# Expanding cached latents by plain fp32 products instead of three split ones, in a decoder step

## Chip, cores and metric

One core of one Trainium2 chip runs the whole program. The time is device microseconds of an execution; three runs of the kernel before are given, and one further execution was profiled.

## What is computed

Two trunk layers of a hybrid decoder are run for 256 prompt tokens and for 8 samples of 8 new tokens each (320 tokens in all). A layer has four mixers side by side (A: latent attention, B: convolution, C: spatial gating, D: a delta-rule recurrence), then cross attention to a memory, then a gated feed-forward. The change lies in mixer A of the samples. There every new query looks at a cache of 2048 past positions, kept as pages of 128 latent rows with 128 numbers each:

```
def mla_expand(ckv, p):
    k_nope = rmsnorm((ckv @ p['mla_w_uk']).reshape(*lead, MLA_HEADS, QK_NOPE), p['mla_gk_nope'])
    v = (ckv @ p['mla_w_uv']).reshape(*lead, MLA_HEADS, V_DIM)
...
    def page_step(carry, phys):
        kn_p, v_p = mla_expand(ckv_p, p)
        sp = mla_scores(q_nope, q_pe, kn_p, kpe_p)
        m_new = jnp.maximum(m, jnp.max(sp, axis=-1, keepdims=True))
...
```

The keys of a page are the latents times a 128x256 matrix, normalised for each head of 64. Only the norms need that product itself: the scores are taken from the latents directly, by queries that were multiplied with the same matrix once.

## The kernel before

The program is written through a framework whose scheduler orders the instructions of each engine from their dependences and its own estimates; each engine then works through its list in that order, and semaphores hold it where a result is missing. `in_order` (L380) keeps the big dense products in their written order, `hold` (L387) keeps an instruction back in the schedule alone.

Dense products use a split: a number is kept as a high part (an fp32r cast, ScalarE) and a low part (the rest, VectorE or GpSimd), and a product is the sum of high by high, high by low and low by high, each a fast fp32r product (`split`, L479; `dense_T`, L513). Activations are split once for each norm in `norm_pre` (L562): for each of the 8 column blocks of the residual stream `x`, one tile `h` of high and low parts (names Nh, Xh and Fh in the profile: before the mixers, before the cross attention, before the feed-forward; six norms in two layers).

The scan over the cache is `mla_sample` (L1298). It has 8 steps a layer: four rounds over the pages, each for two groups of 4 samples. For one step `scan` (L1311) does this:

- It loads 16 page numbers into registers of SP, and SP then issues 16 loads of 64 KB: four tiles `ckt` of 128 x 512 (Sckt in the profile: the latents, transposed, of four pages of one sample). The ring has 12 such tiles, three steps. GpSimd gathers the same pages as rows by four indirect loads (Scb).
- For each of the four tiles ScalarE makes the high part (Sckh, L1336) and GpSimd the low part (Sckl, L1337).
- For each half `u` of the 256 key columns and each tile `j`, three products into a bank pS make the expansion, and ScalarE squares it into Ssq (L1350). The weights uh and ul (Auk) are the split key matrix, made once a layer (L1301 to L1304).
- Narrow products (pZ, L1353) sum the squares over each head: weights of 128 x 32, the squares as 512 moving columns. Each writes 32 of the 128 partitions, so the four tiles `j` fill four quarters of PE's columns and can run at once.
- Four more narrow products (pZ, L1356) of the same form give the scores, from queries and the unsplit Sckt.
- Logarithm, exponentials and a correction step (Sz, Sra; ScalarE and VectorE) turn the sums into inverse norms and scale the scores.

```
                for j in range(4):
                    mm(pn[32 * j : 32 * j + 32], C("hsum")[:, 32 * u : 32 * u + 32], sqs[j], u == 0, u == 1)
            p = ps("Z")
            for j in range(4):
                mm(p[32 * j : 32 * j + 32], qf(4 * g + j), cks[j])
```

`attend` (L1402) then adds the rotary part of the scores (pA from Scb), takes the running softmax, transposes the weights (pA from Sra) and multiplies them with the page rows (pA from Scb and Ak). The scan of the next step is written ahead of the attend of this one, and side work is put between steps: the convolution (Bkeep, pE), the spatial gating (Ccv) and the ends of the other mixers. Banks of PSUM: three for pS, two for pZ, two for pK (the memory's keys and values, `mem_proj`, L1459, which loads memT and weights through the ring wr of three tiles on SP's queue).

## Time and profile before

| | |
|---|---|
| median of 3 runs | 1381.34 us |
| lowest, highest | 1374.33, 1381.94 us |
| span of the profiled execution | 1383.1 us |
| PE, VectorE, ScalarE, GpSimd busy | 1330.9, 962.2, 651.6, 217.5 us |
| the two scans | 191 to 333 us, 886 to 1029 us |
| the two feed-forward stretches | 484 to 716 us, from 1150 us |

The profiled execution has no time of its own beside its span, which runs from the program's first to its last instruction; the span stands 1.8 us above the median of the runs. In the profile a plain fp32 product shows as two records, an fp32r product as one. A record's length includes the way through the array, so records overlap, and the rate of products is read from the distance of their starts.

### The profile page before, as it was taken

How to read it: one execution, taken by the hardware profiler on the slowest of the kernel's cores; microseconds unless marked ns; L12 is line 12 of the kernel's file. 1: busy time of each engine (PE TensorE's matmuls, PEld its weight loads, DVE VectorE, ACT ScalarE, POOL GpSimd, SP SyncE). 2: the span in 40 equal slices, each digit the busy share in tenths (PEclk: the TensorE clock that was granted, in tenths of full speed). 3: DMA queues.
4: the chain of work that ended last, by engine and by line, in shares of the span. 5: the costliest groups of instructions: out<-in, count | busy, mean ns of one | idle time of the engine just before them, and what ended most of it. 6: DMA issues, size and time to landing. Idle time of an engine off the chain costs nothing.

```text
span 1383.1 us, 25248 instructions
## 1 busy us (share of the span) xinstructions
PE 1330.9 (96%) x9032; PEld 1113.5 (81%) x9032; DVE 962.2 (70%) x2414; ACT 651.6 (47%) x1425; POOL 217.5 (16%) x280
## 2 busy tenths in 40 slices
PE   5999999999999999999999899999999989999998
PEld 5859765566796799999998597755668959999998
DVE  6879468767786666566786894698777957655663
ACT  4443236667554544434444432375674635442441
POOL 1201313553000000000012113135540000000000
PEclk9999799999999999999999997999999999999999
DMA  7320313454475544444652204134563823444433
GB/s 233 125 77 15 118 44 89 140 159 145 146 253 191 177 157 145 154 153 151 201 171 94 81 11 123 42 88 133 162 215 143 296 93 137 147 144 153 153 115 107
DMA packets 105486, 189.52 MB, mean 137 GB/s; under 512 B 21393, under 2 KB 58642, under 8 KB 105362
## 3 DMA queue, kind: packets, MB, share of 16 engines
q1 hardware_dynamic: 91040, 157.84, 34.6%
q0 software_dynamic: 5120, 20.98, 5.0%
q10 hardware_dynamic: 9202, 9.11, 2.3%
q8 instruction: 71, 1.16, 0.3%
q14 instruction: 53, 0.43, 0.1%
HBM read 182.12 MB, written 5.75 MB: 136 GB/s over the span
## 4 chain that ended last, share of the span: by engine, by line
PE 52%; issue 9%; DVE 2%; POOL 1%; DMA 1%; ACT 0%; SPq 0%; POOLq 0%; ACTq 0%
PE pD L375 38%; PE pR L375 5%; PE pS L375 2%; PE pA L375 2%; PE pZ L375 2%; PE pA L460 1%; DMA Sckt<-in_ckvT 1%; PE pR L460 0%; DVE Bkeep L401 0%; DVE u L401 0%; PE pE L460 0%; POOL Sckl L397 0%; DVE Ccv L401 0%; DVE u L397 0%; DVE Sz L401 0%
## 5 line engine op out<-in xcount | busy, mean ns | idle before, releaser
L482 ACT CAST wh<-wr 128x512 fp32r<-128x512 f32 (+1 forms) x448 | 252.4, 601 | 133.0 <-PE pD L375 83.9
L375 PE MATMUL pD<-Fh,wh 128*128 128x320 f32 x1408 | 310.5, 309 | 0.0
L397 DVE TENSOR_TENSOR wl<-wr,wh 128x512 fp32r<-128x512 f32 (+1 forms) x448 | 291.7, 674 | 11.4 <-ACT wh L482 9.8
L375 PEld LDWEIGHTS pD<-Fh,wh 128*128 128x128 f32 x1408 | 235.7, 188 | 0.0
L375 PE MATMUL pD<-Fh,wl 128*128 128x320 f32 x704 | 217.5, 309 | 0.0
L375 PE MATMUL pD<-u,wh 128*128 128x320 f32 x704 | 154.9, 309 | 0.0
L375 PEld LDWEIGHTS pD<-Fh,wl 128*128 128x128 f32 x704 | 132.2, 188 | 0.0
L375 PEld LDWEIGHTS pD<-u,wh 128*128 128x128 f32 x704 | 117.8, 188 | 0.0
L397 DVE TENSOR_TENSOR Ff<-pD,fix 128x320 f32<-128x320 f32 x88 | 43.2, 491 | 103.3 <-PE pD L375 100.9
L375 PE MATMUL pD<-u,wl 128*128 128x320 f32 x352 | 108.8, 309 | 0.0
L375 PE MATMUL pD<-Nh,wh 128*128 128x320 f32 x384 | 94.6, 326 | 13.8 <-ACT wh L482 13.8
L413 ACT ACTIVATE u<-Ff 128x320 fp32r<-128x320 f32 x44 | 20.8, 472 | 176.1 <-DVE Ff L397 176.1
L397 POOL TENSOR_TENSOR Sckl<-Sckt,Sckh 128x512 fp32r<-128x512 f32 x64 | 85.8, 1351 | 108.7 <-ACT Sckh L1336 91.7
L375 PE MATMUL pS<-Sckh,Auk 128*128 128x512 f32 x256 | 92.0, 432 | 4.3 <-DVE Sra L401 1.8
L413 ACT ACTIVATE Ssq<-pS 128x512 f32<-128x512 f32 x128 | 73.5, 594 | 45.3 <-PE pS L375 38.6
L397 DVE TENSOR_TENSOR fix<-fix,pD 128x320 f32<-128x320 f32 x80 | 38.8, 485 | 73.0 <-PE pD L375 72.3
L375 PEld LDWEIGHTS pD<-Nh,wh 128*128 128x128 f32 x384 | 66.8, 194 | 19.6 <-ACT wh L482 13.8
L375 PEld LDWEIGHTS pS<-Sckh,Auk 128*128 128x128 f32 x256 | 47.3, 197 | 36.4 <-issue 22.1
L401 DVE SCALAR_TENSOR_TENSOR Bkeep<-Bkeep,fix 128x256 f32<-128x256 f32 x120 | 74.5, 624 | 0.6
L1326 POOL DMA_INDIRECT Scb<-in_ckv,fix x64 | 63.4, 991 | 63.4 <-PE pR L375 23.3
L375 PE MATMUL pZ<-Ssq,fix 128*32 128x512 f32 x256 | 71.9, 654 | 1.3 <-ACT Sra L414 0.9
L375 PEld LDWEIGHTS pD<-u,wl 128*128 128x128 f32 x352 | 66.1, 188 | 0.0
(478 smaller groups left out, 2580.7 us busy)
## 6 DMA issues: line engine op xcount, KB each, us to landing
wr<-in_w SPq DMA_DIRECT2D x200, 512.0 KB
Sckt<-in_ckvT SPq DMA_DIRECT2D x256, 64.0 KB
u<-in_memK SPq DMA_DIRECT2D x32, 256.0 KB
u<-in_memV SPq DMA_DIRECT2D x32, 256.0 KB
wr<-in_w SPq DMA_DIRECT2D x16, 384.0 KB
wr<-in_memT SPq DMA_DIRECT2D x12, 256.0 KB
wr<-in_w SPq DMA_DIRECT2D x8, 352.0 KB
Rmk<-in_cst ACTq DMA_DIRECT2D x2, 704.0 KB
```

The source lines that it names most:

```text
L375: return T.matmul(out, lhsT=lhsT, rhs=rhs, start=start, stop=stop)
L397: return (eng or V).tensor_tensor(out=out, in0=in0, in1=in1, op=op)
L401: return V.scalar_tensor_tensor(out=out, in0=in0, scalar=scalar, in1=in1, op0=op0, op1=op1)
L413: return S.activation(out, in_, func, bias=bias, scale=scale)
L460: T.transpose(out, in_, ident[:n, :n])
L482: S.copy(hi, src)
L1326: ld = nc.gpsimd.indirect_dma_start(out=cb.rearrange("p i c -> p (i c)"), out_offset=None, in_=a["ckv"], in_offset=off)
```

## The change

In the scan the casts, the low parts, their tiles (Sckh, Sckl) and the split key matrix (Auk) go; each expansion is one plain fp32 product of the unsplit weights `ukv` (in the profile a part of Akeep) and the unsplit tile Sckt. The register loads of a step are held, in the schedule, to the scores of the second step before instead of the low parts of the third. In `norm_pre` the eight tiles of split activations become columns of one tile, and the rings Nh, Fh and Xh have one buffer of eight times the size. Comments and docstrings that the diff also drops are left out here.

```
-    BUFS = dict(u=13, wr=3, wh=4, wl=4, Nh=8, Nf=2, Nsm=2, Fh=8, Ff=4, Fsm=2, Xh=8, Xm=5, Xf=2, Xk2=2, Xcc=2, Xsm=8, Yk2=2, Ycc=2, Ysm=2,
+    BUFS = dict(u=13, wr=3, wh=4, wl=4, Nh=1, Nf=2, Nsm=2, Fh=1, Ff=4, Fsm=2, Xh=1, Xm=5, Xf=2, Xk2=2, Xcc=2, Xsm=8, Yk2=2, Ycc=2, Ysm=2,
...
         hs = []
+        hall = sb("h", [128, 8, 2, NT], F32R)
         for k in range(8):
-            h = sb("h", [128, 2, NT], F32R)
+            h = hall[:, k]
             split(h[:, 0], h[:, 1], x[k], gain[:, k : k + 1])
             hs.append(h)
...
-        u2 = sb("uk", [128, 2, 256], F32R)
-        uh, ul = u2[:, 0], u2[:, 1]
-        hold(S.copy(uh, ukv[:, 0:256]), pages[0])
-        tt(ul, ukv[:, 0:256], uh.bitcast(F32), SUB)
...
-        lows = []
+        base = len(scored)
...
             for ld in loads:
-                hold(ld, lows[-BUFS["Sckt"]] if len(lows) >= BUFS["Sckt"] else cpage)
+                hold(ld, scored[-2] if len(scored) - base >= 2 else cpage)
...
                 ck = ck.rearrange("p n t -> p (n t)")
                 cks.append(ck)
-                hi, lo = sb("ckh", [128, 512], F32R), sb("ckl", [128, 512], F32R)
-                S.copy(hi, ck)
-                lows.append(tt(lo, ck, hi.bitcast(F32), SUB, G if j in [0, 1, 2, 3] else V))
-                ckhl.append((hi, lo))
...
                 for j in range(4):
                     p = ps("F")
-                    hi, lo = ckhl[j]
-                    mm(p, uh[:, us], hi, True, False)
-                    mm(p, ul[:, us], hi, False, False)
-                    mm(p, uh[:, us], lo, False, True)
+                    mm(p, ukv[:, us], cks[j])
                     sq = sb("sq", [128, 512])
                     act(sq, p, AF.Square)
```

The scheduler orders the lists anew. PE, the fifth step of the second layer's scan, before: pS are the expansions, pZ<-Ssq the sums of squares.

```order
L375 MATMUL pS<-Sckh_10949,Auk_10012 128x512 x2
L375 MATMUL pS<-Sckl_10950,Auk_10012 128x512
L375 MATMUL pS<-Sckh_10960,Auk_10012 128x512 x2
L375 MATMUL pS<-Sckl_10961,Auk_10012 128x512
L375 MATMUL pS<-Sckh_10971,Auk_10012 128x512 x2
L375 MATMUL pS<-Sckl_10972,Auk_10012 128x512
L375 MATMUL pS<-Sckh_10982,Auk_10012 128x512 x2
L375 MATMUL pS<-Sckl_10983,Auk_10012 128x512
L375 MATMUL pZ<-Ssq_10991,fix 32x512
L375 MATMUL pZ<-Ssq_10997,fix 32x512
L375 MATMUL pZ<-Ssq_11003,fix 32x512
L375 MATMUL pZ<-Ssq_11009,fix 32x512
```

Here four expansions stand together, and their four narrow products behind them. The same step on PE in the changed kernel; pE belongs to the spatial gating, pK to the memory's keys, pA to the step before, and pZ<-Sckt are the scores:

```order
L375 MATMUL pS<-Sckt_10526,Akeep_9039 128x512
L375 MATMUL pE<-Ccv_10438 128x64 x2
L375 MATMUL pE<-Ccv_10438 64x64 x4
L375 MATMUL pZ<-Ssq_10555,fix 32x512
L375 MATMUL pS<-Sckt_10533,Akeep_9039 128x512
L375 MATMUL pZ<-Sckt_10526,Akeep_9039 32x512
L460 MATMUL pA<-fix,Sra_10198 128x128 x4
L375 MATMUL pS<-Sckt_10540,Akeep_9039 128x512
L375 MATMUL pZ<-Ssq_10559,fix 32x512
L375 MATMUL pZ<-Sckt_10533,Akeep_9039 32x512
L375 MATMUL pZ<-Sckt_10540,Akeep_9039 32x512
L375 MATMUL pK<-wh,Mh_11494 128x512
```

Narrow products stand between the expansions now, one or three at a time, and some of the scores have moved ahead of the sums of squares.

SP's queue in the first layer, at the start of the eighth group of page loads, before (a row ISA sets the address of the load below it):

```order
L1332 DMA Sckt_3455<-in_ckvT 128x128
L1317 TENSOR_LOAD pt_65
L1332 ISA
L1332 DMA Sckt_3757<-in_ckvT 128x128
L1332 ISA
```

The memory's first load follows only behind all of that group. In the changed kernel it stands behind the fourth group, ahead of the fifth:

```order
L1329 DMA Sckt_2597<-in_ckvT 128x128
L1457 DMA wr<-in_memT 128x512
L510 DMA wr<-in_w 128x1024
L1314 TENSOR_LOAD pt_65
L1329 ISA
L1329 DMA Sckt_2793<-in_ckvT 128x128
```

So two loads of the memory's projection were moved past four groups of page loads.

## Rows read from the trace of the kernel before

**Rows 1.** The page: busy us, share of the span and instructions of each engine.

```profile
PE 1330.9 (96%) x9032; PEld 1113.5 (81%) x9032; DVE 962.2 (70%) x2414; ACT 651.6 (47%) x1425; POOL 217.5 (16%) x280
```

**Rows 2.** Stages: window, length, busy us of each engine, granted clock, DMA share, GB/s.

```profile
191.00:333.00 142.00, 135.50 (x950) 81.13 (x949) 109.50 (x261) 91.19 (x214) 64.95 (x60) 0.95 0.42 122
...
886.00:1029.00 143.00, 134.17 (x946) 80.29 (x946) 113.15 (x260) 92.48 (x213) 66.15 (x55) 0.95 0.49 140
```

**Rows 3.** What PE waited for, first scan, then second: us, times, longest.

```profile
PE pS L375 <- DVE Sra L401: 1.0, 1, 1.0
...
PE pS L375 <- ACT Sckh L1336: 0.6, 1, 0.6
...
PE pE L460 <- issue: 0.3, 1, 0.3
...
PE pA L375 <- DVE Ak L1419: 3.2, 1, 3.2
...
PE pE L460 <- issue: 0.2, 1, 0.2
```

**Rows 4.** The chain that ended last, second scan, shares of the window by line.

```profile
by line: PE pS L375 23.5%; PE pZ L375 21.7%; PE pA L375 14.9%; issue 9.6%; DMA Sckt<-in_ckvT 6.3%; DVE Bkeep L401 3.2%; PE pA L460 2.8%; POOL Sckl L397 2.7%; DVE Ccv L401 2.3%; PE pE L460 2.2%; DVE Sz L401 1.5%; SPq L1332 1.3%; DVE Ccv L397
```

**Rows 5.** Timeline of PE, old expansions: start us, us, engine, line, tiles, form, records.

```profile
925.86 0.62 PE L375 MATMUL pS<-Sckh,Auk 128*128 128x512 f32 x2
926.32 0.39 PE L375 MATMUL pS<-Sckl,Auk 128*128 128x512 f32 x1
926.55 0.62 PE L375 MATMUL pS<-Sckh,Auk 128*128 128x512 f32 x2
927.02 0.40 PE L375 MATMUL pS<-Sckl,Auk 128*128 128x512 f32 x1
927.25 0.62 PE L375 MATMUL pS<-Sckh,Auk 128*128 128x512 f32 x2
```

**Rows 6.** Timeline of PE around a plain fp32 product of the new shape.

```profile
83.11 0.40 PE L375 MATMUL pD<-wh,Nh 128*64 128x512 f32 x1
83.34 1.02 PE L375 MATMUL pA<-Akeep 128*128 128x512 f32 x2
83.80 0.80 PE L375 MATMUL pD<-wh,Nh 128*64 128x512 f32 x1
```

**Rows 7.** Timeline of PE, narrow products in groups of four.

```profile
923.21 1.06 PE L375 MATMUL pZ<-Ssq,fix 128*32 128x512 f32 x8
924.10 1.03 PE L375 MATMUL pZ<-Sckt,Akeep 128*32 128x512 f32 x6
```

**Rows 8.** Timeline of PE, a narrow product alone.

```profile
929.32 0.40 PE L375 MATMUL pS<-Sckl,Auk 128*128 128x512 f32 x1
929.71 1.04 PE L375 MATMUL pZ<-Ssq,fix 128*32 128x512 f32 x2
930.69 0.48 PE L375 MATMUL pA<-Akeep,As 64*128 64x128 f32 x2
```

**Rows 9.** Squares, casts, low parts: ns min/median/max, first and last start; then a wait.

```profile
L413 ACT ACTIVATE Ssq<-pS x128: 571/597/616, 194.0 to 1025.0; 128x512 f32<-128x512 f32 x128
L1336 ACT CAST Sckh<-Sckt x64: 600/611/637, 161.5 to 1005.2; 128x512 fp32r<-128x512 f32 x64
L397 POOL TENSOR_TENSOR Sckl<-Sckt,Sckh x64: 1263/1292/1732, 162.2 to 1008.9; 128x512 fp32r<-128x512 f32 x64
...
  DMA Sckt<-in_ckvT: 9.1, 4
```

**Rows 10.** Timeline of VectorE at the start: the low parts of a norm.

```profile
9.95 3.78 DVE L401 SCALAR_TENSOR_TENSOR Nh<-fix,Nh 128x320 fp32r<-128x320 f32 x8
```

More of the change, by code (lines that the diff above doesn't have):

```diff
@@ L1300, in mla_sample @@
         oT = t["take"](4, 64)
-        u2 = sb("uk", [128, 2, 256], F32R)
-        uh, ul = u2[:, 0], u2[:, 1]
-        hold(S.copy(uh, ukv[:, 0:256]), pages[0])
-        tt(ul, ukv[:, 0:256], uh.bitcast(F32), SUB)
         qf = lambda b: qp[:, b].rearrange("p h t -> p (h t)")
         PG = [0, 0, 3, 3]
-        lows = []
+        base = len(scored)
         def scan(g, Q):
             ch[0] = "S"
-            cbs, cks, ckhl = [], [], []
+            cbs, cks = [], []
             cpage = pages[[0, 2, 3, 3][min(2 * Q + g, 3)]]
```

## Prediction, made before the changed kernel ran

> **What bounds the kernel now.** Read the busy shares first: TensorE (PE) is busy 96% of a span of 1383.1 us, VectorE 70%, ScalarE 47%, GpSimd 16% [rows 1]. A busy share says little of what ends a stage, so next come the stages. The change touches two of them, one in each layer: the scan over the cached pages, from 191 to 333 us and from 886 to 1029 us. There PE is busy 135.5 of 142 us and 134.2 of 143 us, and the mean granted clock is 0.95 [rows 2]: between the two levels, 2.4 and 1.2 GHz, that is some 14 us of each scan at the lower one, or 7 us of full-speed time lost in each. Third, what PE itself waited for in these two stretches: nine rows in each, the first and last shown, which add up to 5.6 us in the first and 8.8 us in the second [rows 3]. So about 14 us out of 285 are PE waiting for another engine; the rest is PE working through its list in order, with short gaps where it goes from one kind of product to another. Two things then decide the change: how long PE takes for one expansion by the old and by the new way, and what stands around it in PE's order. The chain that ended last in the second scan says the same: products on pS, pZ and pA hold 60% of it, but 18.6% lie with the page loads, the low parts on GpSimd and gaps in issue [rows 4]; that is the best argument for a rival below.
>
> **The change, part by part.**
>
> *Products.* A scan step expands four tiles of 512 latents by two halves of the key weights: 8 expansions a step, 8 steps a layer, 2 layers, so 128. Each was three products of split (fp32r) operands. Where they follow one another they start at 925.86, 926.55 and 927.25 us: one expansion every 0.69 us [rows 5]. The new one is one plain fp32 product of the same shape, 128x128 weights by 512 columns. The trace has eight records of that shape, two for each product (the new tokens' latents against all 512 columns of the two expansion weights). One starts at 83.34 us; its two records end 1.02 us later, and the next product, 0.80 us long in its record, ends at 84.60 us, while its neighbour of the same kind takes 0.40 us: so it could not begin to stream before 84.20 us. One plain product holds PE for 0.86 us [rows 6]. The difference is 0.17 us, and 128 x 0.17 = 21.8 us more PE time. Bounds: 0 if the new products overlap with their neighbours in a way that these eight records don't show, and 128 x (1.02 - 0.69) = 42 us if nothing can start before the two records have ended. I take 21.8, since the rows are of this very shape.
>
> *Order of PE.* The narrow products (pZ) each fill a quarter of PE's columns. Four side by side take as long as one: eight records, four products, start at 923.21 us and the next four at 924.10, that is 0.89 us [rows 7]. One alone starts at 929.71 us and the next instruction at 930.69 us: 0.98 us [rows 8]. So what counts is not how many there are (96 a layer, before and now) but in how many groups they stand. Counted in PE's order over a scan, where a group is what can run side by side in an unbroken run, there were 35 in each layer; now there are 44 in the first and 48 in the second. The pieces of order printed above show why: the plain expansion is scheduled as one long instruction, and single pZ products are put between expansions. That is 22 groups more, 22 x 0.98 = 21.6 us. Bounds: 0 if each stands where PE would have waited anyway, and 25 us if each also pays the 0.16 us between the end of the wide product before it (929.32 + 0.23 us) and its start. I take 21.6.
>
> The Trainium skill, "TensorEngine Tiling (Array Packing)", Key Properties, says that changing the tiling mode, not merely the tile, drains TensorE. The gaps of 0.16 us ahead of a lone narrow product and 0.12 us behind it agree; by that rule each added group would cost 1.14 us and the sum would be some 3.5 us higher.
>
> *What no longer has to be made.* 64 casts of 611 ns leave ScalarE (39 us) and 64 subtractions of 1.29 us leave GpSimd (83 us) [rows 9], besides two small ones for the weights. Neither engine is the bound: in the scans ScalarE is busy 91 of 142 us and GpSimd 65 [rows 2]. What this pays is only what PE waited for them. Of the waits in [rows 3] one row names the cast, 0.6 us. But ScalarE and GpSimd also feed what VectorE and the squares on ScalarE do, and other rows name those. Bounds: 1 us if only the cast's wait goes, 14.4 us if all of PE's waits in both scans go. I take half, 7.2 us. What is late next is the square of an expansion (597 ns on ScalarE [rows 9]) before its pZ product: one expansion now comes out every 0.86 us instead of 0.69, so squares keep up. Where a lone pZ product does wait for its square, the next expansions stand behind it on PE, and their squares, the scores and the step's softmax behind those.
>
> *Loads.* Each tile of latents is still read by the last pZ product of its step, so buffers of the page loads come free as before. What moves is on SP's queue: in the first layer the first load for the memory's keys (256 KB, and 512 KB of weights behind it) stood behind all eight groups of page loads and stands now behind the fourth. The page loads of four steps are queued behind it. All waits of GpSimd for a page load were 9.1 us in four times [rows 9]; nothing says they reach PE. Bounds: a gain of 9 us to a loss of 9 us; I take nothing. The DMA engines are busy at 0.42 and 0.49 there [rows 2], which is cover enough.
>
> *Split activations in one tile.* The eight splits of a norm write columns of one tile. The first dense products wait for ScalarE and VectorE at the same places in the order as before, so I take nothing. If a product had to wait for all eight, the price would be at most the 3.78 us in which VectorE makes the eight low parts [rows 10], at six norms, 23 us; below nothing there is no reason to go, since the same instructions run.
>
> *Sum.* 21.8 + 21.6 - 7.2 = 36.2 us on a profiled span of 1383.1 us, that is 1419. That span is 1.8 us above the median of the runs, so against the median 1381.3 + 36 = 1417 us.
>
> **The rivals.**
>
> *The added groups are hidden* (0.18). A lone pZ product is put where PE has nothing ready. If it always fills a wait, the 21.6 us fall away: 21.8 - 7.2 = +14.6, 1396 us. For it: the short gaps that PE has at every change of product. Against it: PE's own waits in both scans are 14.4 us in all, fewer than the groups need.
>
> *The split is what paces the scan* (0.09), the case that ends not slower. Place: the head of each step, where a page load lands, is cast, then subtracted, and only then multiplied. In the chain of the second scan the loads, the low parts and the issue gaps hold 6.3 + 2.7 + 9.6 = 18.6% of 143 us, 26.6 us [rows 4]; the same in the first scan makes 53.2. If all that goes, 43.4 - 53.2 = -9.8 us, 1371. It decides as soon as more than 43.4 us of the two scans hang on it. Against it: PE stood still for only 14.4 us of the 285 [rows 3], so most of that chain ran beside PE's work.
>
> *More waits than now* (0.18). Narrow products between wide ones each wait for a square, the memory's loads hold page loads up by the 9.1 us above, and each added group pays its 0.16 us: 36.2 + 9.1 + 3.5 = +48.8, 1430 us. For it: the finer order has more places where PE, which does not reorder products, can wait. Against it: less is asked of ScalarE and GpSimd.
>
> **How the numbers follow.** The forecast, 1417 us, has 0.55. The low end of the range lies under the second case (1396), by some of the 14 us that the lower clock costs in both scans; the high end over the last (1430): 1390 to 1436 us. The runs shown spread by 0.55%, so about 1%, 13.8 us, can be told from no change: below 1367.5 is faster, above 1395.2 slower. Slower takes the forecast, the last rival and two thirds of the second, 0.85; within 1% takes the rest of the second and two thirds of the case of the split, 0.12; faster is what is left of that, 0.03.
>
> **What would show it.** Right: pS has 256 records (two per product) that follow each other by 0.43 us; pZ pairs that stand alone, 0.98 us each, in greater number; both scans longer by some 18 us; the feed-forward stretches, 484 to 716 us and after 1150, as long as before. Wrong: scans of the same length or shorter with PE gaps gone (the split paced them); plain products closer than 0.86 us; longer stages outside the scans (the one tile of activations made products wait, or the clock fell elsewhere); a granted clock in the scans far from 0.95.

## The result and the profile after

The changed kernel takes 1399.39 us (median of 4 runs, 1398.14 to 1405.14) against 1378.58 us for the kernel before in the same comparison (4 runs, 1374.33 to 1381.94): ratio 1.0154, 95% interval 1.0121 to 1.0187, so +20.8 us. The forecast was +36 us, 1417 us, with a range from 1390 to 1436. The profiled execution after has a span of 1397.0 us (its own time 1398.76), 13.9 us over the span of before. The span of before lies 4.5 us above the median of this comparison, so the two profiles show a smaller difference than the runs.

The page of the kernel after, busy us, share of the span and instructions of each engine:

```profile
PE 1353.5 (97%) x8904; PEld 1083.2 (78%) x8904; DVE 925.3 (66%) x2412; ACT 632.4 (45%) x1359; POOL 129.2 (9%) x216
```

Against [rows 1] GpSimd has lost 88 us, 82.7 of them its 64 subtractions, and ScalarE 19 us. VectorE has lost 37 us too, and nothing was taken from it but one small subtraction a layer. That was in nobody's sum, and it turns out to matter.

The stages of the kernel after (window, length, busy us of each engine, granted clock, DMA share, GB/s): the two scans from the first expansion to the last score, and the first feed-forward stretch.

```profile
192.60:341.90 149.30, 145.03 (x891) 67.52 (x890) 92.56 (x269) 84.19 (x198) 29.81 (x29) 0.99 0.45 129
888.80:1037.90 149.10, 146.54 (x880) 66.67 (x878) 91.47 (x265) 82.42 (x191) 30.05 (x27) 1.00 0.44 131
484.00:716.00 232.00, 231.27 (x1579) 230.94 (x1578) 161.58 (x325) 104.76 (x194) 3.76 (x18) 1.00 0.50 164
```

The same stretches of the kernel before, cut at its own first expansion and last score:

```profile
191.30:332.60 141.30, 135.07 (x948) 80.83 (x946) 109.12 (x259) 90.79 (x213) 64.36 (x54) 0.95 0.42 122
884.20:1027.40 143.20, 134.60 (x950) 81.20 (x948) 113.15 (x260) 92.03 (x212) 64.92 (x53) 0.95 0.49 141
```

The scans took 284.5 us and now take 298.4: +13.9, as much as the two spans differ by. That is in part an effect of the cut. In the changed order five sums of squares and the last record of an expansion stand behind the last score, before the change none. The same two stretches with their tails, that is, taken on to the first product of the cross attention, before and then after:

```profile
191.30:406.30 215.00, 205.89 (x1421) 141.21 (x1420) 163.83 (x393) 134.26 (x308) 69.83 (x60) 0.95 0.47 145
884.20:1083.70 199.50, 189.68 (x1370) 130.18 (x1369) 159.27 (x377) 126.55 (x290) 70.08 (x58) 0.97 0.48 145
```

```profile
192.60:409.30 216.70, 211.71 (x1351) 124.52 (x1350) 142.74 (x389) 122.72 (x278) 33.61 (x33) 0.99 0.48 149
888.80:1097.20 208.40, 204.80 (x1300) 115.31 (x1299) 134.44 (x374) 114.08 (x262) 33.08 (x30) 1.00 0.42 133
```

With the tails the difference is 10.7 us (10.6 by the rounded windows), and the other 3.2 us lie elsewhere. The granted clock rose from 0.95 to 0.99 and 1.00 in the scans.

Where these differences come from can be worked out from PE's records in the stretches. Each instant counts for the product that was in the array first; a record is taken 0.17 us shorter than printed, since a lone fast product prints 0.40 us and the next starts after 0.23 [rows 5]; time at the lower clock counts half as work, and the other half stands in a line of its own; what no product fills is a gap.

| both scans, us | before | after | change | change with the tails | forecast |
|---|---|---|---|---|---|
| expansions (pS) | 91.8 | 113.4 | +21.6 | +22.4 | +21.8 |
| narrow products (pZ) | 75.8 | 87.6 | +11.8 | +15.6 | +21.6 |
| other products | 66.9 | 65.4 | -1.5 | -4.1 | 0 |
| gaps of PE | 37.9 | 30.3 | -7.6 | -10.0 | -7.2 |
| lost to the lower clock | 12.1 | 1.7 | -10.4 | -13.2 | 0 |
| length | 284.5 | 298.4 | +13.9 | +10.7 | +36.2 |

The levels lean on the 0.17 us, the changes hardly: with 0.16 us the gaps are 32.9 and 25.8 us, and the changes -7.1 us of gaps and +20.7 us on pS.

PE's timeline of the kernel after, second scan (start us, us, tiles, form, records):

```profile
955.62 1.02 PE L375 MATMUL pS<-Sckt,Akeep 128*128 128x512 f32 x2
956.58 1.04 PE L375 MATMUL pZ<-Ssq,fix 128*32 128x512 f32 x2
957.55 1.13 PE L375 MATMUL pS<-Sckt,Akeep 128*128 128x512 f32 x2
```

This is what the forecast pictured: an expansion of two records, a narrow product alone for 0.97 us [rows 8], the next expansion. The waits of PE that answer to the second half of [rows 3] have shrunk to three rows:

```profile
PE pZ L375 <- ACT Ssq L413: 1.3, 1, 1.3
PE pA L375 <- ACT Am L1267: 1.0, 2, 0.7
PE pS L375 <- DMA Sckt<-in_ckvT: 0.2, 1, 0.2
```

In the first scan such rows add up to 4.3 us, against 5.6 before. Over both scans they fall from 14.4 to 6.8 us, by as much as the gaps.

The chain that ended last in the second scan, for [rows 4]:

```profile
by line: PE pS L375 38.3%; PE pZ L375 29.2%; issue 21.0%; PE pA L375 18.1%; PE pA L460 3.2%; PE pE L460 2.1%; PE pE L375 1.9%; POOL Scb L1323 1.3%; PE pK L375 1.2%; PE pR L460 0.7%; ACT Am L1267 0.4%; DVE Sra L401 0.4%; PE pR L375 0.4%; ACT
```

The 21.0% of issue is nearly all one piece of 30.1 us that starts at 1037.4 us, at the window's end; inside the window issue is some 1%, and for that piece the shares add up to more than 100%. The page loads (6.3%), GpSimd's low parts (2.7%) and VectorE's Bkeep and Ccv (3.2 and 2.3%) have left the chain, and PE's own products have taken their place: the scan is bound by PE's list and little else.

**VectorE beside GpSimd.** The 37 us that VectorE lost are found in one kind of row. An operation of the convolution, among the instructions on the tile Bkeep in the trace before (count, ns min/median/max, first and last start):

```profile
L401 DVE SCALAR_TENSOR_TENSOR Bkeep<-Bkeep,fix x120: 443/475/3360, 175.7 to 985.1; 128x256 f32<-128x256 f32 x120
```

Two operations on Sra in the same trace:

```profile
L401 DVE SCALAR_TENSOR_TENSOR Sra<-pZ,Sra x16: 675/680/691, 218.2 to 1028.7; 128x512 f32<-128x512 f32 x16
...
L401 DVE SCALAR_TENSOR_TENSOR Sz<-Sra,Sz x16: 672/680/2293, 219.5 to 1029.5; 128x512 f32<-128x512 f32 x16
```

After, on Bkeep and on Sz:

```profile
L401 DVE SCALAR_TENSOR_TENSOR Bkeep<-Bkeep,fix x120: 447/477/486, 177.4 to 973.4; 128x256 f32<-128x256 f32 x120
```

```profile
L401 DVE SCALAR_TENSOR_TENSOR Sz<-Sra,Sz x16: 676/683/689, 219.1 to 1052.4; 128x512 f32<-128x512 f32 x16
```

The medians agree; the maxima have gone from 3360 to 486 ns and from 2293 to 689. The row with an operand in a PSUM bank (pZ) never had them. In the two scans of before, 45 operations of VectorE last over 0.15 us longer than the fast tenth of their own kind, 44.8 us together, and 44.7 of these lie beside a subtraction of GpSimd (Sckl). Of the operations that start under such a subtraction, none of the 15 with a PSUM operand is stretched, 33 of the 44 elementwise ones with two tensors in SBUF are, and so are all three with one tensor and scalars (TENSOR_SCALAR). After the change the excess is 0.2 us. The Trainium skill says this in "SBUF — State Buffer", Who interferes with whom: a VectorE instruction with two SBUF inputs and a GpSimd instruction that reads SBUF use one port in common, and the second to come stands still until the first has ended. The counts agree in which operations with two inputs are hit; that rule does not speak of the three with one tensor.

One place shows how this reached PE. VectorE in the trace before, second scan:

```profile
947.20 0.48 DVE L401 SCALAR_TENSOR_TENSOR Ccv<-Ccv,Csm 128x256 f32<-128x256 f32 x1
947.59 3.36 DVE L401 SCALAR_TENSOR_TENSOR Bkeep<-Bkeep,fix 128x256 f32<-128x256 f32 x1
...
951.74 2.91 DVE L401 SCALAR_TENSOR_TENSOR Ccv<-Ccv,Csm 128x256 f32<-128x256 f32 x2
954.57 1.48 DVE L397 TENSOR_TENSOR Ccv<-Ccv 128x256 f32<-128x256 f32 x1
955.97 0.67 DVE L1419 COPY Ak<-pA 128x512 f32<-128x512 f32 x1
```

GpSimd beside it:

```profile
948.13 2.53 POOL L397 TENSOR_TENSOR Sckl<-Sckt,Sckh 128x512 fp32r<-128x512 f32 x2
951.46 4.31 POOL L397 TENSOR_TENSOR Sckl<-Sckt,Sckh 128x512 fp32r<-128x512 f32 x3 [0.80 <-DMA Sckt<-in_ckvT]
```

And PE:

```profile
952.41 1.05 PE L375 MATMUL pZ<-Ssq,fix 128*32 128x512 f32 x2
956.70 0.66 PE L375 MATMUL pA<-Scb,Ak 128*32 128x128 f32 x8 [3.24 <-DVE Ak L1419]
```

Two subtractions run from 948.13 to 950.66 us, and VectorE's operation of 0.48 us ends at 950.95; three more run from 951.46 to 955.77, and three operations of half a microsecond take 1.5 each. The short copy Ak, which PE wants, stands behind them, and PE waits 3.24 us: the row of 3.2 in [rows 3]. The wait is put down to the copy and to VectorE; its cause is on a third engine. The order of arrival can't be read from these rows: VectorE's record starts at 947.59 us, 0.54 us ahead of the first subtraction, and still ends behind both.

**The clock.** What stands behind that wait, in windows of the kernel before (busy us in the order PE, PEld, DVE, ACT, POOL, then granted clock, DMA share, GB/s):

```profile
950.00:955.30 5.30, 3.46 (x12) 1.24 (x11) 5.30 (x7) 2.87 (x6) 4.43 (x4) 1.00 0.14 45
955.30:962.10 6.80, 5.40 (x54) 3.45 (x55) 4.59 (x12) 1.58 (x3) 3.07 (x4) 0.50 0.20 51
962.10:970.00 7.90, 7.90 (x54) 5.49 (x53) 5.03 (x13) 4.04 (x10) 1.23 (x2) 1.00 0.67 205
```

PE stood still from 953.46 to 956.70 us, the last 1.8 us of the first window and the first 1.4 us of the second, and the whole second window, 6.8 us, is at the lower level (0.50, 1.2 GHz). Each of the five such stretches in the scans of before, 27.3 us in all (12.1 us of work lost), begins behind gaps of PE, or in one, of which the longest was 0.8 to 3.4 us. After the change there is one, 3.4 us long, behind gaps of 0.8 and 0.5 us. Not every wait brings one: the longest gap in the scans after, 1.5 us around the wait of 1.3 us above, was followed by none.

The clock also differs between executions of one kernel. Every run lists its span and its mean granted clock, and the span times (1 - clock) is an estimate of what the lower level cost it. In four sets of 9 to 19 executions of the kernel before, which ran beside the experiments, this loss averages 36.5 to 41.2 us, and in four executions of the kernel after 26.6 us. With it taken off, the 15 executions of the first set scatter by 1.4 us (standard deviation) instead of 4.0, and the kernel after stands 27 to 31 us above the sets of before. At an equal clock the change is dearer than 20.8 us, and the clock gives a third to a half of that back.

### The profile page after: what moved, and what is told of

It reads as the page before. It is cut to its first block, busy times and chain, and to the rows that moved or that the text cites. A ratio compares the mean times of both kernels' runs of the same rounds, so it can differ in the third digit from the quotient of the medians.

```text
span 1397.0 us, 24604 instructions
## 1 busy us (share of the span) xinstructions
PE 1353.5 (97%) x8904; PEld 1083.2 (78%) x8904; DVE 925.3 (66%) x2412; ACT 632.4 (45%) x1359; POOL 129.2 (9%) x216
## 3 DMA queue, kind: packets, MB, share of 16 engines
q8 instruction: 70, 1.15, 0.3%
## 4 chain that ended last, share of the span: by engine, by line
PE 85%; issue 8%; DVE 3%; POOL 1%; DMA 1%; ACT 1%; SPq 0%; POOLq 0%; DVEq 0%; ACTq 0%
PE pD L375 48%; PE pR L375 10%; PE pS L375 8%; PE pZ L375 7%; PE pA L375 5%; PE pK L375 2%; PE pA L460 2%; PE pX L375 1%; PE pR L460 1%; PE pE L460 1%; PE pE L375 1%; DVE u L401 1%; PE pY L375 1%; DMA Bkeep<-in_convh 1%; DMA wr<-in_memT 0%
## 5 line engine op out<-in xcount | busy, mean ns | idle before, releaser
L482 ACT CAST wh<-wr 128x512 fp32r<-128x512 f32 (+1 forms) x448 | 261.2, 604 | 272.6 <-PE pD L375 211.9
L375 PE MATMUL pS<-Sckt,Akeep 128*128 128x512 f32 x256 | 131.1, 622 | 1.0 <-PE pZ L375 0.8
L397 DVE TENSOR_TENSOR Ff<-pD,fix 128x320 f32<-128x320 f32 x88 | 43.3, 492 | 66.8 <-PE pD L375 61.2
L375 PEld LDWEIGHTS pS<-Sckt,Akeep 128*128 128x128 f32 x256 | 42.8, 192 | 54.9 <-issue 37.6
L375 PE MATMUL pZ<-Ssq,fix 128*32 128x512 f32 x256 | 80.6, 603 | 3.0 <-ACT Ssq L413 1.7
L397 DVE TENSOR_TENSOR fix<-fix,pD 128x320 f32<-128x320 f32 x80 | 38.8, 485 | 51.6 <-PE pD L375 50.9
L375 PE MATMUL pD<-Nh,wl 128*128 128x320 f32 x192 | 62.4, 325 | 2.3 <-DVE wl L397 2.3
L413 ACT ACTIVATE u<-Ff 128x320 fp32r<-128x320 f32 x44 | 20.8, 472 | 88.7 <-DVE Ff L397 88.7
L375 PE MATMUL pD<-wh,Nh 128*128 128x352 f32 (+3 forms) x192 | 58.8, 378 | 0.2 <-ACT u L413 0.2
```

What stands on the lines that cost most here:

```text
L375: return T.matmul(out, lhsT=lhsT, rhs=rhs, start=start, stop=stop)
L397: return (eng or V).tensor_tensor(out=out, in0=in0, in1=in1, op=op)
L413: return S.activation(out, in_, func, bias=bias, scale=scale)
L482: S.copy(hi, src)
```

## Experiments

Ratios are to runs of the kernel before on the same chip; the kernel after stands at 1.0154. "Groups" are runs of narrow products that can stand side by side, counted in PE's order; by this count before has 35 and 35, after 45 and 49. Splits of time (pS, pZ, gaps, lower clock) are worked out as in the table above.

**One more fast product.** The kernel before, with the first of the three products of an expansion issued twice; the output is that of three.

```
+                    mm(p, uh[:, us], hi)
                     mm(p, uh[:, us], hi, True, False)
```

> The kernel before with the first of the three split products issued twice, so that an expansion holds PE for four times 0.23 us, about as long as the plain product, while casts and low parts stay. PE's work grows by 128 x 0.23 = 29 us. Theory (a PE with more to do in the scans keeps the higher clock): time at 1.2 GHz in the scans falls from 27 to under 10 us and gaps by some 5, so 1393 to 1400 us. Rival (the clock came back because the casts and low parts, and PE's waits for them, were gone): time at 1.2 GHz stays near 27 us and the time is 1406 us or more.

Measured: 1413.13 us, 1.0239 (1.0195 to 1.0284): the rival. The expansions take 120.9 us instead of 91.8: 128 products at 0.23 us. But 26.6 us of the scans are still at the lower clock, and the gaps are 41.7 us. More work for PE does not bring the clock back while the waits stay.

**Casts and low parts kept.** The kernel after, in which ScalarE and GpSimd still make the high and low parts, which nothing reads.

```
                 cks.append(ck)
+                hi, lo = sb("ckh", [128, 512], F32R), sb("ckl", [128, 512], F32R)
+                S.copy(hi, ck)
+                tt(lo, ck, hi.bitcast(F32), SUB, G)
```

> The changed kernel, but ScalarE still casts each tile of latents and GpSimd still makes its low part, and nobody reads them. Theory (PE's own list sets the scans, the removed casts and low parts were beside it): 1399 to 1404 us, at most 4 us of the scans at 1.2 GHz. Rival (what the change saves in gaps and clock comes from ScalarE and GpSimd having less to do): 1410 to 1420 us, gaps of PE in the scans back from 30 to 38 us and the time at 1.2 GHz back from 3 to 27 us.

Measured: 1405.28 us, 1.0178 (1.0131 to 1.0224), not to be told from after: 1 us over the theory's range, under the rival's. VectorE's excess beside GpSimd is back at 26.8 us, PE's gaps rise from 30.3 to 34.0 us and the lower clock stays at 3.4 us. So 26.8 us of stretched operations go with only 3.7 us of gaps: in the order of after they mostly stand where PE does not wait for them.

**The one tile alone.** The kernel before with only the split activations in one tile; the rings have one buffer, as in the change.

```
...
+        hall = sb("h", [128, 8, 2, NT], F32R)
         for k in range(8):
-            h = sb("h", [128, 2, NT], F32R)
+            h = hall[:, k]
```

> The kernel before with only the split activations in one tile. Theory (the tile costs nothing, all of the change lies in the scans): 1379 us, ratio to before 1.000 within 0.004, both scans as long as before (141 and 143 us). Rival (products wait for the whole tile, or the other layout of the memory delays a stage): 1385 us or more, with the added time ahead of the dense products of a norm.

Measured: 1370.01 us, 0.9925 (0.9893 to 0.9956): faster, against both theories. PE's work in the scans is the same (234.8 us against 234.5), the gaps are 32.3 us instead of 37.9 and the lower clock 6.8 us instead of 27.3. The tile changes the scheduler's lists of all engines by some places within the scans. At the place shown above VectorE has the same operations in the same order, but GpSimd's subtractions fall on others of them: from the sum in Sra to the copy Ak it is 8.4 us instead of 11.6, and PE does not wait there. The stretching as such is still there, 40.0 us over 44 operations in the scans, against 44.8 us over 45. Over the six executions the loss to the clock is 26.5 us, against 36.5 in the 15 of before beside them, and with it taken off both kernels take the same, 1343.8 and 1343.3 us: the gain in time is the clock's. That the order, and not something in the tile, is the cause is argued from the trace. The next run bears on it.

**The change without the one tile.** The kernel after with eight tiles again, and eight buffers for them.

```
...
-        hall = sb("h", [128, 8, 2, NT], F32R)
         for k in range(8):
-            h = hall[:, k]
+            h = sb("h", [128, 2, NT], F32R)
```

> The kernel after, but with the split activations in eight tiles as before: the plain products, their order and the held page loads without the one tile. In PE's order the narrow products stand in 47 and 49 groups (after, by the same count, 45 and 49; before 35 and 35). Theory: the parts add up. The one tile alone gave 0.9925 of the time before, so this kernel should be some 10 us slower than the one after, 1.019 to 1.026 of the time before (1405 to 1414 us). Rival: the one tile's 10 us were no gain of its own but came from waits and a lower clock that only the order of before had, and the plain products' order does not have them anyway: then the time is that of after within 4 us, 1.012 to 1.018.

Measured: 1398.29 us, 1.0116 (1.0078 to 1.0154): the rival, just under its range. Within the change the tile gives nothing that can be measured. Scans of 297.8 us with gaps of 28.3 and 3.4 us at the lower clock are those of after. The 10 us on the kernel before were not the tile's own.

**Narrow products held together.** The kernel after, with sums of squares and scores held in the schedule behind the last square of each half.

```
-                    act(sq, p, AF.Square)
+                    last = act(sq, p, AF.Square)
...
-                    mm(pn[32 * j : 32 * j + 32], C("hsum")[:, 32 * u : 32 * u + 32], sqs[j], u == 0, u == 1)
+                    hold(mm(pn[32 * j : 32 * j + 32], C("hsum")[:, 32 * u : 32 * u + 32], sqs[j], u == 0, u == 1), last)
...
-                mm(p[32 * j : 32 * j + 32], qf(4 * g + j), cks[j])
+                hold(mm(p[32 * j : 32 * j + 32], qf(4 * g + j), cks[j]), last)
```

> The changed kernel with the narrow products of a half, and the scores, held in the schedule until the fourth square, so that PE's order has 30 and 29 groups of narrow products instead of 45 and 49. Theory (each added group costs PE time, by the trace of after some 0.45 us each): 35 fewer groups, 16 us less on PE, part given back in waits for the fourth square: 1385 to 1393 us. Rival (single narrow products only filled PE's waits): 1399 us or more.

Measured: 1375.07 us, 0.9954 (0.9922 to 0.9986), 30 and 29 groups, against 1.0154, and better than the theory's range. The pZ time falls from 87.6 to 58.5 us, 29.1 us for 35 groups, 0.83 us each (0.93 with the tails), though 17.1 us of the scans are at the lower clock again in the profiled execution, which had the lowest granted clock of the ten (0.970 to 0.981). So the groups are not hidden.

**Who made the groups.** The kernel before with only the new hold on the register loads of a step.

```
-                hold(ld, lows[-BUFS["Sckt"]] if len(lows) >= BUFS["Sckt"] else cpage)
+                hold(ld, scored[-2] if len(scored) - base >= 2 else cpage)
```

> The kernel before with one part of the change only: the register loads of a step's page numbers are held, in the schedule, to the scores of the second step before, in place of the low parts of the third. Nothing else is edited. Yet the scheduler's PE order has 43 and 49 groups of narrow products instead of 35 and 35. Theory: this hold, which the prediction priced at nothing, is what splits the groups; 22 groups at the 0.54 us that each cost in the kernel after (11.8 us for 22) make +12 us, 1.006 to 1.012 of the time before, with more than 83 us on pZ in the two scans together (76 before). Rival: page loads and their hold cost nothing, as predicted, and the groups are hidden here: 0.997 to 1.003.

Measured: 1418.37 us, 1.0255 (1.0217 to 1.0293), +35 us, three times the theory's 12. The pZ time goes from 75.8 to 90.4 us, but the gaps also grow, from 37.9 to 57.9. With the tails the two stretches are 33.3 us longer: 17.4 us of gaps, 14.7 on pZ and 5.2 on pS more, 4.0 less lost to the clock. PE's waits in the second scan, first rows:

```profile
PE pS L375 <- POOL Sckl L397: 3.7, 6, 1.2
PE pA L460 <- DVE As L397: 3.1, 1, 3.1
PE pZ L375 <- ACT Ssq L413: 1.0, 2, 0.7
```

PE waits for GpSimd's low parts six times. That loads scheduled about a step later leave less time for cast and subtraction is the reading that fits; it was not tried alone. The edit that the prediction priced at nothing is, on the kernel before, dearer than the whole change.

The same question in the kernel after: the loads held earlier.

```
-                hold(ld, scored[-2] if len(scored) - base >= 2 else cpage)
+                hold(ld, firsts[-3] if len(firsts) >= 3 else cpage)
...
-                    mm(p, ukv[:, us], cks[j])
+                    m1 = mm(p, ukv[:, us], cks[j])
+                    if u + j == 0:
+                        firsts.append(m1)
```

> The kernel after with one edit: the register loads are held to the first expansion of the third step before, which stands about where the low part stood that before named, in place of the scores of the second step before. In PE's order the groups fall from 45 and 49 to 35 and 38. Theory: the groups come from the loads' hold and not from the length of the plain products; 21 groups by 0.54 us, and less single work, give 1383 to 1391 us, 1.003 to 1.009 of the time before. Rival: the order was made by the longer plain products, and the groups left or gone are hidden beside other quarter products: 1396 to 1403 us, 1.013 to 1.018.

Measured: 1385.23 us, 1.0032 (1.0005 to 1.0058). Its two scans:

```profile
191.90:332.20 140.30, 137.23 (x890) 65.44 (x889) 93.12 (x271) 82.14 (x197) 28.81 (x29) 0.99 0.46 136
885.50:1027.60 142.10, 139.32 (x890) 66.48 (x890) 91.53 (x264) 80.00 (x189) 29.74 (x27) 0.99 0.51 153
```

They are 16 us shorter than those of after, all of it pZ: 71.0 us instead of 87.6, below the 75.8 of before. The expansions still take 113.5 us. So the long plain products did not split the groups; the held loads did, and they cost about 17 us of the 21 (1.0154 against 1.0032; the two intervals allow 11 to 23 us). Unlike the one tile's 10 us this is not the clock's: with the loss to the clock taken off, the difference is 17.8 us.

Both together, the early loads and the held narrow products:

```
+                hold(ld, firsts[-3] if len(firsts) >= 3 else cpage)
...
+                hold(mm(p[32 * j : 32 * j + 32], qf(4 * g + j), cks[j]), last)
```

> The kernel after with both of its order faults taken away: the register loads held to the first expansion of the third step before (this alone gave 1385 us), and the narrow products of a step held, in the schedule, behind the last square of each half. Groups in PE's order 32 and 33 (35 and 38 without the second hold, 45 and 49 after). Theory: time on pZ falls from 71 to 58 to 62 us, some 11 us more, and waits stay at 27 us: 1369 to 1378 us, 0.990 to 0.998 of before, about as the hold of the narrow products alone (1375). Rival: held narrow products come late for the softmax behind them, and the waits take back what the groups give: 1382 us or more.

Measured: 1380.78 us, 0.9974 (0.9951 to 0.9997). The pZ time is 61.5 us as expected, but the gaps are 33.5 us instead of 27.1 and the lower clock 9.4 instead of 6.8. The time lies between the two ranges, nearer to the rival's. In the profiled execution, 3.9 us above the median, most of what the groups gave went into waits; by the medians some 8 us of it were kept (1.0032 against 0.9974).

**Who stretches VectorE.** The kernel before with the low parts on VectorE.

```
-                lows.append(tt(lo, ck, hi.bitcast(F32), SUB, G if j in [0, 1, 2, 3] else V))
+                lows.append(tt(lo, ck, hi.bitcast(F32), SUB, V))
```

> The kernel before with the 64 low parts of the latents made by VectorE instead of GpSimd. In the trace of before, VectorE's operations that lie beside GpSimd's subtractions last 44.7 us longer in the two scans than the same operations elsewhere; in the trace of after that excess is 0.2 us. Here 64 subtractions come to VectorE (some 0.69 us each by its other operations of that shape with two inputs, 44 us), so that its busy time in the scans stays about the same. Theory: what made PE wait were single operations of VectorE stretched to 1.5 to 3.4 us in the way of short results; without them PE's gaps in the two scans fall from 38 to 32 us or less, and the time is 0.993 to 0.998 of before. Rival: the waits come from the length of VectorE's queue, whoever fills it: gaps of 36 us or more, 0.999 to 1.006.

Measured: 1367.59 us, 0.9885 (0.9850 to 0.9920), better than the theory's range. The rows of its low parts and then of Bkeep:

```profile
L397 DVE TENSOR_TENSOR Sckl<-Sckt,Sckh x64: 669/682/715, 165.6 to 999.8; 128x512 fp32r<-128x512 f32 x64
```

```profile
L401 DVE SCALAR_TENSOR_TENSOR Bkeep<-Bkeep,fix x120: 467/476/493, 177.6 to 999.4; 128x256 f32<-128x256 f32 x120
```

VectorE does 64 operations more, and 43.6 us more work, yet nothing is stretched any longer. The scans:

```profile
188.90:320.50 131.60, 128.91 (x936) 78.37 (x934) 103.27 (x286) 89.03 (x209) 30.51 (x27) 1.00 0.46 131
878.30:999.10 120.80, 118.96 (x876) 74.10 (x874) 95.83 (x267) 82.82 (x194) 27.76 (x30) 1.00 0.48 138
```

The granted clock is 1.00 in both. Part of the second scan's last work has moved behind its end, so compare scans with their tails: 414.4 us before, 394.9 here; gaps 50.7 and 41.0 us, lost to the lower clock 14.9 and 0, PE's work 348.9 and 353.9. The 19.5 us come from gaps and clock; outside, 4.8 us go back, 3.2 of them to the lower clock. Over the five executions the loss to the clock is 24.9 us, against 38.8 in the runs of before beside them, and with it taken off both kernels stand at 1342.5 us: here too the gain in time is the clock's. The order changed as well (39 and 37 groups for 35 and 35). So this run shows that GpSimd's subtractions are what stretches VectorE; that the stretch is what cost the 1.15% is argued from the one wait traced above.

The same with narrow products held as above (30 and 30 groups):

```
+                lows.append(tt(lo, ck, hi.bitcast(F32), SUB, V))
...
+                hold(mm(p[32 * j : 32 * j + 32], qf(4 * g + j), cks[j]), last)
```

> The kernel before with the low parts on VectorE (alone 0.9885) and the narrow products of a step held behind the last square of each half: 30 and 30 groups in PE's order against 39 and 37 with the low parts on VectorE alone. Nothing of the change is in it. Theory: 16 groups fewer at 0.54 to 0.98 us each, 9 to 15 us, so 1350 to 1360 us, 0.977 to 0.983 of before, the fastest of both ways of expanding. Rival: the split way has less slack on ScalarE and VectorE, so products held back wait for squares that queue behind casts: 1364 us or more.

Measured: 1379.95 us, 0.9956 (0.9934 to 0.9978): the rival. PE's work in scans and tails falls by 20.7 us, but the gaps are 53.7 us and the lower clock 37.5. Over the nine executions the loss to the clock is 43.3 us, and the rest is 11.6 us less than before: the theory's 9 to 15 us are there, and the clock takes them back. Its waits in the second scan, first rows, and one stretch behind such a wait:

```profile
PE pS L375 <- DVE Sckl L397: 3.0, 1, 3.0
PE pE L460 <- DVE Bg L397: 2.0, 1, 2.0
```

```profile
1003.00:1006.50 3.50, 1.26 (x6) 0.66 (x4) 3.17 (x7) 0.98 (x4) 0.00 (x0) 1.00 0.00 0
1006.50:1013.30 6.80, 6.05 (x45) 4.58 (x46) 4.60 (x12) 2.94 (x8) 0.15 (x1) 0.50 0.00 0
```

**A version that beats both.** Split expansions, low parts on VectorE, narrow products held, and the sums of squares as full products with weights `hz`, padded by zeros. The squares are rounded to the fast format, which is a part of the computation that differs.

```
...
-                    sq = sb("sq", [128, 512])
+                    sq = sb("sq", [128, 512], F32R)
...
-                    mm(pn[32 * j : 32 * j + 32], C("hsum")[:, 32 * u : 32 * u + 32], sqs[j], u == 0, u == 1)
+                    hold(mm(pn, hz[:, u, j], sqs[j], u + j == 0, u + j == 4), last)
```

> As the run before this one (split expansions, low parts on VectorE, narrow products held), but the sums of squares are eight products a step with weights padded by zeros to 128 columns, in the fast format, in place of eight narrow plain fp32 products; for this the squares are rounded to that format when ScalarE writes them. Theory: PE's time is what counts, and eight full products of 0.23 us (1.84 us a step, in any order) take the place of two or more groups of 0.9 us or more, so the pZ time falls from about 58 to 45 us: 1338 to 1350 us, 0.968 to 0.977 of before. Rival: full products cannot run beside the quarter products of other tags, and what those hid comes out: 1355 to 1365 us.

Measured: 1356.14 us, 0.9792 (0.9763 to 0.9822), the fastest of all runs. The pZ time falls to 49.7 us, from 57.9, but the quarter products of Scb that had run beside narrow ones take 41.7 instead of 35.1 us: the rival's mechanism, and its time. Without the hold, on these products and on the scores:

```
...
-                    hold(mm(pn, hz[:, u, j], sqs[j], u + j == 0, u + j == 4), last)
+                    mm(pn, hz[:, u, j], sqs[j], u + j == 0, u + j == 4)
```

> Split expansions, low parts on VectorE and the eight full-width sums of squares from rounded squares, as in the last run, but without the hold of narrow products. Theory: the hold is what brought back waits of 2 to 3 us and the lower clock behind them (scans with their tails: gaps 50 us, 17 us at the lower clock; with the low parts on VectorE alone 41 and none), and full-width sums do not need it: gaps 38 to 43 us, 1338 to 1350 us, 0.966 to 0.975 of before. Rival: without the hold full and quarter products alternate more often, and the scan does not get shorter: 1353 to 1362 us.

Measured: 1362.96 us, 0.9826 (0.9793 to 0.9859), gaps 47.5 us with the tails: the rival again. The intervals of the two overlap; the hold makes no difference that can be told here.

## Why the prediction was right, point by point

The direction held and the time lies in the range, at a bit over half of the forecast's loss. At 1399.4 us it stands nearer to the rival of the hidden groups (1396) than to the forecast (1417), though it came there another way: two terms of the sum were too high, and both misses point down. Of the signs that were named, the plain products and the lone narrow ones came as described; the scans grew by 8.0 and 5.9 us and not by some 18 each, and the granted clock left 0.95 for 0.99 and 1.00, which stood among the signs of being wrong.

*Products*: right. +21.6 us against 21.8. What was read from eight records in another stage [rows 6] held for 128 products.

*Order of PE*: the mechanism was right, its size and its author were not. The added groups, 22 by the prediction's count and 24 by the one used here, cost 11.8 us up to the last score and 15.6 with the tails, 0.5 to 0.7 each, not 21.6. Some lone narrow products ran beside quarter products of Scb, and those take 29.6 us after and 32.4 before; that is 3 us, and where the rest of the difference lies was not traced. In the run with held narrow products a group gave more, 0.83 to 0.93 us. By the rule of the Trainium skill that the prediction weighed ("TensorEngine Tiling (Array Packing)", Key Properties) and the gap that it read in its rows, a group was 1.14 us; these sums lie further from it than from 0.98. And the text said that "the plain expansion is scheduled as one long instruction", which should have split the groups; with the loads held early the plain products leave 35 and 38 groups.

*Loads*: wrong. "I take nothing", within 9 us either way. I looked at the memory's loads on SP's queue and not at what a hold does to the scheduler's whole order. It costs about 17 us of the change, and 35 us alone on the kernel before. In the sum this cost stood under the order of PE, which is why the sum came out better than this term.

*What no longer has to be made*: right in size, -7.6 us of gaps against -7.2 (-10.0 with the tails), by luck: it was half of a bound. "PE waited for them" was read as waits for ScalarE and GpSimd; another way, which the longest wait shows, is that GpSimd's subtractions held VectorE's operations up. How much of the 7.6 us came that way stays open: with 26.8 us of stretching brought back the gaps grew by 3.7 us, and with 40.0 us of it in place the one tile alone had 5.6 us less of gaps than before.

*The granted clock*: this term is what failed, with 10.4 us in the profiled scans and 10 to 15 us over all executions. The sum has no line for it; "some of the 14 us that the lower clock costs in both scans" went into the low end of the range alone. Stretches at 1.2 GHz stood behind PE's waits, so a wait that goes can be worth more than its length. Here 7.6 us of gaps and 10.4 us of lost clock went together; that more work alone does not do it was shown by the run with one more product.

*One tile*: nothing, as told, within the change. But "below nothing there is no reason to go" was false as a statement about the edit: on the kernel before, it was 10 us faster, by way of the clock.

*Rivals*: that the split paces the scan had more in it than 0.09. The loads and low parts of [rows 4] did leave the chain; what went in the scans is 18 us, gaps and clock, not 53, and it did not come back with the casts and subtractions alone (3.7 us of gaps, no clock), so it hangs on what PE waits for and not on that work as such. With the loads held early the 21.7 us more on pS meet 10.8 us less of gaps, 8.8 less lost to the clock and 4.8 less on pZ: 1.0032. The hidden groups were half true.

## What to carry to other kernels

An edit that only holds an instruction in the schedule, or renames tiles, is an edit of every engine's order: count what stands in the new order, and undo each such line alone before the main edit is blamed or praised. When a wait is put down to a short operation, look what stood before it on its engine, and compare min and max of the same shape: a maximum of seven times the median pointed to another engine here. Look at the granted clock behind each wait of PE before the wait is priced by its length, and at that of every execution: two gains of 10 to 15 us in this kernel were the clock's alone.

## What the runs showed of the hardware that was not expected

Operations of VectorE with two SBUF inputs lasted up to 3.36 us instead of 0.48 beside subtractions on GpSimd, which themselves took 1.29 us [rows 9], and operations with a PSUM operand did not. The same 64 subtractions on VectorE took 0.68 us each and stretched nothing. Most of the spread between executions of the kernel before is the granted clock, 0.967 to 0.981 in 15 of them: with the loss to it taken off, 4.0 us of standard deviation become 1.4. More work on PE (29 us of extra products) left the time at the lower clock where it was, 27.3 and 26.6 us; in seven kernels with gaps of 25 to 34 us it fell to between 0 and 9.4 us, but the kernel after with held narrow products kept 17.1 us of it with gaps of only 27.2 us, behind gaps of 1.1, 2.0 and 1.2 us. The sum of the gaps does not decide it, and what does stays open.
